# Interleaving two arrays in place: three large buffers, 32 KiB load rows and 64 KiB store rows

## The chip, the cores and the metric

One core of one Trainium2 chip runs the kernel; nothing else runs on the chip. The metric is the device time of an execution in microseconds (us). The profile's span is about 2 us shorter than that time (317.6 against 319.8 us for the kernel before). The experiments ran on several chips, each beside the kernel before, whose medians were 319.56 to 319.86 us. Its executions agree within 0.3%; those of some kernels below do not, which turns out to be part of the story.

## The reference

```python
batch, seq, dim = 32, 256, 1024          # x, y: fp32
result = np.zeros((batch, seq, dim * 2), dtype=np.float32)
result[..., 0::2] = x
result[..., 1::2] = y
```

As flat arrays, out[2i] = x[i] and out[2i+1] = y[i]. There are 67.11 MB to read and 67.11 MB to write, and no arithmetic.

## The kernel before

Loads of x and y go through one queue (issued by the engine SP), stores through another (issued by ACT). VectorE copies each input to every second element of a separate output tile. `P` is 128 partitions; each partition's part of a transfer is one contiguous row. The load rows hold 4096 elements (16 KiB), the store rows 2 x 2048 (16 KiB), and small tiles end the kernel.

```python
WL = 4096
WS = 2048
xpool = ctx.enter_context(tc.tile_pool(name="xp", bufs=3))
ypool = ctx.enter_context(tc.tile_pool(name="yp", bufs=3))
opool = ctx.enter_context(tc.tile_pool(name="op", bufs=6))
lwidths = [WL] * (total // P // WL - 1) + [2048, 1024, 512, 256, 256]
for lw in lwidths:
    ...                                   # tiles and access patterns
    nc.sync.dma_start(out=xtile, in_=xs)
    nc.sync.dma_start(out=ytile, in_=ys)
    soff = 0
    while soff < lw:
        ...
        nc.vector.tensor_copy(out=otile[:, 0::2], in_=xsub)
        nc.vector.tensor_copy(out=otile[:, 1::2], in_=ysub)
        nc.scalar.dma_start(out=os_, in_=otile)
        ...
```

Of the kernel before, what the change touches and what calls it, by code (L numbers as in the profile page):

```python
# [2 lines left out]

# [4 lines left out]


@with_exitstack
def kernel(
    ctx: ExitStack,
    tc: tile.TileContext,
    x: bass.AP,
    y: bass.AP,
    out: bass.AP,
):
    nc = tc.nc
    P = 128  # L20

    total = 1
    for s in x.shape:
        total *= s

    WL = 4096
    WS = 2048

    xf = x.rearrange("b s d -> (b s d)")
    yf = y.rearrange("b s d -> (b s d)")  # L30
    of = out.rearrange("b s d -> (b s d)")

    fp32 = mybir.dt.float32

    xpool = ctx.enter_context(tc.tile_pool(name="xp", bufs=3))
    ypool = ctx.enter_context(tc.tile_pool(name="yp", bufs=3))
    opool = ctx.enter_context(tc.tile_pool(name="op", bufs=6))

    lwidths = [WL] * (total // P // WL - 1) + [2048, 1024, 512, 256, 256]
    assert sum(lwidths) == total // P  # L40

    start = 0
    k = 0
    for lw in lwidths:
        xtile = xpool.tile([P, WL], fp32, name="xtile")[:, :lw]
        ytile = ypool.tile([P, WL], fp32, name="ytile")[:, :lw]

        xs = dataclasses.replace(xf, offset=start, ap=[[lw, P], [1, lw]])
        ys = dataclasses.replace(yf, offset=start, ap=[[lw, P], [1, lw]])
        nc.sync.dma_start(out=xtile, in_=xs)  # L50
        nc.sync.dma_start(out=ytile, in_=ys)  # L51

        soff = 0
        while soff < lw:
            width = min(WS, lw - soff)
            otile = opool.tile([P, 2 * WS], fp32, name="otile")[:, : 2 * width]
            os_ = dataclasses.replace(
                of,
                offset=2 * start + 2 * soff,
                ap=[[2 * lw, P], [1, 2 * width]],  # L60
            )
            xsub = xtile[:, soff : soff + width]
            ysub = ytile[:, soff : soff + width]
            if False:
                nc.gpsimd.tensor_copy(out=otile[:, 0::2], in_=xsub)
                nc.gpsimd.tensor_copy(out=otile[:, 1::2], in_=ysub)
            else:
                nc.vector.tensor_copy(out=otile[:, 0::2], in_=xsub)  # L68
                nc.vector.tensor_copy(out=otile[:, 1::2], in_=ysub)  # L69
            nc.scalar.dma_start(out=os_, in_=otile)  # L70
            k += 1
            soff += width

        start += P * lw
    assert start == total


# [1 line left out]
_INS = ['x', 'y']  # L79
_OUTS = [((32, 256, 2048), 'float32')]  # L80


# [23 lines left out]
```

## Time and profile before

| | before |
|---|---|
| time, median of runs | 319.79 us (319.71 to 320.22) |
| span of the profiled run | 317.6 us |
| rate over the span | 423 GB/s |
| VectorE busy | 76.8 us (24%) |
| DMA packets | 10,802 |

A page is read from the span down. "Busy" is an engine's own work. The line of digits for DMA is the mean busy share of sixteen DMA engines in 40 slices of the span, in tenths; the GB/s below counts bytes at the start of the packet that moves them, so with long packets single slices jump about (from 370 to 479 after the first and before the last slice of the changed kernel). The queue lines give packets, megabytes and the time of the packets as a share of sixteen engines' span; q1 carries the loads, q10 the stores. A packet here is one record of the trace: one row of a transfer, or a small one at its end (q1 of the kernel before has 5760, which is 40 loads of 128 rows and 16 small ones). The prediction shows these lines and reads them.

### The profile page before, as it was taken

How to read it: one execution, taken by the hardware profiler on the slowest of the kernel's cores; microseconds unless marked ns; L12 is line 12 of the kernel's file. 1: busy time of each engine (PE TensorE's matmuls, PEld its weight loads, DVE VectorE, ACT ScalarE, POOL GpSimd, SP SyncE). 2: the span in 40 equal slices, each digit the busy share in tenths (PEclk: the TensorE clock that was granted, in tenths of full speed). 3: DMA queues.
4: the chain of work that ended last, by engine and by line, in shares of the span. 5: the costliest groups of instructions: out<-in, count | busy, mean ns of one | idle time of the engine just before them, and what ended most of it. 6: DMA issues, size and time to landing. Idle time of an engine off the chain costs nothing.

```text
span 317.6 us, 285 instructions
## 1 busy us (share of the span) xinstructions
DVE 76.8 (24%) x70; POOL 0.2 (0%) x4
## 2 busy tenths in 40 slices
DVE  0522112222022221122220222202222202221130
POOL 0000000000000000000000000000000000000000
DMA  8999999999999999999999999999999999999997
GB/s 293 429 396 429 429 431 429 429 429 437 437 435 433 433 429 429 429 429 429 429 431 429 429 429 435 437 437 430 431 431 429 431 429 429 429 432 427 421 423 285
DMA packets 10802, 134.24 MB, mean 423 GB/s; under 512 B 1200, under 2 KB 1712, under 8 KB 2608
## 3 DMA queue, kind: packets, MB, share of 16 engines
q1 hardware_dynamic: 5760, 67.11, 50.0%
q10 hardware_dynamic: 5040, 67.11, 49.4%
q14 instruction: 2, 0.02, 0.0%
HBM read 67.11 MB, written 67.11 MB: 423 GB/s over the span
## 4 chain that ended last, share of the span: by engine, by line
DMA 94%; issue 3%; SPq 1%; DVE 1%
DMA xtile<-in_x_dram 82%; DMA ytile<-in_y_dram 12%; SPq L51 0%; DVE otile L69 0%; SPq L50 0%; DVE otile L68 0%
## 5 line engine op out<-in xcount | busy, mean ns | idle before, releaser
L68 DVE COPY otile<-xtile 128x2048 f32<-128x2048 f32 (+3 forms) x35 | 38.4, 1134 | 118.4 <-issue 94.4
L69 DVE COPY otile<-ytile 128x2048 f32<-128x2048 f32 (+3 forms) x35 | 38.4, 1134 | 117.9 <-DMA ytile<-in_y_dram 117.9
L90 POOL MEMSET const-bfloat16-1.0<- 128x1 bf16 x1 | 0.1, 102 | 0.0
L90 POOL MEMSET const-uint8-127<- 128x1 uint8 x1 | 0.1, 101 | 0.0
L90 POOL MEMSET const-float32-0.0<- 128x1 f32 x1 | 0.1, 99 | 0.2 <-issue 0.2
L90 POOL MEMSET const-float32-1.0<- 128x1 f32 x1 | 0.1, 98 | 0.0
## 6 DMA issues: line engine op xcount, KB each, us to landing
out_dram<-otile ACTq DMA_DIRECT2D x31, 2048.0 KB, 19.5
xtile<-in_x_dram SPq DMA_DIRECT2D x15, 2048.0 KB, 38.8
ytile<-in_y_dram SPq DMA_DIRECT2D x15, 2048.0 KB, 38.8
xtile<-in_x_dram SPq DMA_DIRECT2D x1, 1024.0 KB, 36.4
ytile<-in_y_dram SPq DMA_DIRECT2D x1, 1024.0 KB, 34.0
out_dram<-otile ACTq DMA_DIRECT2D x1, 1024.0 KB, 9.2
xtile<-in_x_dram SPq DMA_DIRECT2D x1, 512.0 KB, 29.0
ytile<-in_y_dram SPq DMA_DIRECT2D x1, 512.0 KB, 30.2
```

The source lines that it names most:

```text
L68: nc.vector.tensor_copy(out=otile[:, 0::2], in_=xsub)
L69: nc.vector.tensor_copy(out=otile[:, 1::2], in_=ysub)
L90: nc = _bacc.Bacc("TRN2", target_bir_lowering=False, num_devices=1)
```

## The change

The intent is fewer and longer transfers. A tile now has 8192 elements a partition, and one 64 KiB buffer holds x in its lower and y in its upper half, then the interleaved result. So that nothing is overwritten before it is read, half of x waits in PSUM and the rest is spread out in copies of halving length. Loads have rows of 32 KiB; a store has rows of 64 KiB, but for the last tile, which is stored in two halves.

```diff
-    WL = 4096
-    WS = 2048
+    W = 8192
+    H = W // 2
+    EDGE = 64
...
+    zpool = ctx.enter_context(tc.tile_pool(name="zp", bufs=3))
+    tpool = ctx.enter_context(tc.tile_pool(name="tp", bufs=1, space=bass.MemoryType.PSUM))
...
+        nc.sync.dma_start(out=z[:, :W], in_=xs)
+        nc.sync.dma_start(out=z[:, W:], in_=ys)
...
+        copy(out=keep, in_=z[:, H:W])                     # half of x to PSUM
+        hi = H
+        while hi > EDGE:
+            lo = hi // 2
+            copy(out=z[:, 2 * lo : 2 * hi : 2], in_=z[:, lo:hi])
+            hi = lo
...
+        copy(out=z[:, 1:W:2], in_=z[:, W : W + H])        # first half of y
...                                                        # second half of y, by halves
+        copy(out=z[:, W : 2 * W : 2], in_=keep)           # back from PSUM
...
+            os_ = dataclasses.replace(of, offset=2 * base, ap=[[2 * W, P], [1, 2 * W]])
+            nc.scalar.dma_start(out=os_, in_=z)           # 64 KiB rows
```

More of the change, by code (lines that the diff above doesn't have):

```diff
@@ L24 @@
         total *= s
-    WL = 4096
-    WS = 2048
+    n = total // (P * W)
+    assert n * P * W == total
     xf = x.rearrange("b s d -> (b s d)")
@@ L33 @@
     fp32 = mybir.dt.float32
-    xpool = ctx.enter_context(tc.tile_pool(name="xp", bufs=3))
-    ypool = ctx.enter_context(tc.tile_pool(name="yp", bufs=3))
-    opool = ctx.enter_context(tc.tile_pool(name="op", bufs=6))
-    lwidths = [WL] * (total // P // WL - 1) + [2048, 1024, 512, 256, 256]
-    assert sum(lwidths) == total // P
-    start = 0
-    k = 0
-    for lw in lwidths:
-        xtile = xpool.tile([P, WL], fp32, name="xtile")[:, :lw]
-        ytile = ypool.tile([P, WL], fp32, name="ytile")[:, :lw]
-        xs = dataclasses.replace(xf, offset=start, ap=[[lw, P], [1, lw]])
-        ys = dataclasses.replace(yf, offset=start, ap=[[lw, P], [1, lw]])
-        nc.sync.dma_start(out=xtile, in_=xs)
-        nc.sync.dma_start(out=ytile, in_=ys)
-        soff = 0
-        while soff < lw:
-            width = min(WS, lw - soff)
-            otile = opool.tile([P, 2 * WS], fp32, name="otile")[:, : 2 * width]
-            os_ = dataclasses.replace(
-                of,
-                offset=2 * start + 2 * soff,
-                ap=[[2 * lw, P], [1, 2 * width]],
-            )
-            xsub = xtile[:, soff : soff + width]
-            ysub = ytile[:, soff : soff + width]
-            if False:
-                nc.gpsimd.tensor_copy(out=otile[:, 0::2], in_=xsub)
-                nc.gpsimd.tensor_copy(out=otile[:, 1::2], in_=ysub)
-            else:
-                nc.vector.tensor_copy(out=otile[:, 0::2], in_=xsub)
-                nc.vector.tensor_copy(out=otile[:, 1::2], in_=ysub)
-            nc.scalar.dma_start(out=os_, in_=otile)
-            k += 1
-            soff += width
-        start += P * lw
@@ L75 @@
-    assert start == total
+    zpool = ctx.enter_context(tc.tile_pool(name="zp", bufs=3))
+    tpool = ctx.enter_context(tc.tile_pool(name="tp", bufs=1, space=bass.MemoryType.PSUM))
+    epool = ctx.enter_context(tc.tile_pool(name="ep", bufs=2))
+    copy = nc.vector.tensor_copy
+    for t in range(n):
+        z = zpool.tile([P, 2 * W], fp32, name="z")
+        base = t * P * W
+        xs = dataclasses.replace(xf, offset=base, ap=[[W, P], [1, W]])
+        ys = dataclasses.replace(yf, offset=base, ap=[[W, P], [1, W]])
+        nc.sync.dma_start(out=z[:, :W], in_=xs)
+        nc.sync.dma_start(out=z[:, W:], in_=ys)
+        keep = tpool.tile([P, H], fp32, name="keep")
+        edge = epool.tile([P, EDGE], fp32, name="edge")
+        copy(out=keep, in_=z[:, H:W])
[4 more added lines that the diff above has]
+            hi = lo
+        copy(out=edge[:, :hi], in_=z[:, :hi])
+        copy(out=z[:, 0 : 2 * hi : 2], in_=edge[:, :hi])
+        copy(out=z[:, 1:W:2], in_=z[:, W : W + H])
+        last = t == n - 1
+        if last:
+            os_ = dataclasses.replace(of, offset=2 * base, ap=[[2 * W, P], [1, W]])
+            nc.scalar.dma_start(out=os_, in_=z[:, :W])
+        k = 0
+        while H - k > EDGE:
+            k1 = k + (H - k) // 2
+            copy(
+                out=z[:, W + 2 * k + 1 : W + 2 * k1 : 2],
+                in_=z[:, W + H + k : W + H + k1],
+            )
+            k = k1
+        edge2 = epool.tile([P, EDGE], fp32, name="edge2")
+        copy(out=edge2[:, : H - k], in_=z[:, W + H + k : 2 * W])
+        copy(out=z[:, W + 2 * k + 1 : 2 * W : 2], in_=edge2[:, : H - k])
+        copy(out=z[:, W : 2 * W : 2], in_=keep)
+        if last:
+            os_ = dataclasses.replace(of, offset=2 * base + W, ap=[[2 * W, P], [1, W]])
+            nc.scalar.dma_start(out=os_, in_=z[:, W:])
+        else:
+            os_ = dataclasses.replace(of, offset=2 * base, ap=[[2 * W, P], [1, 2 * W]])
+            nc.scalar.dma_start(out=os_, in_=z)
```

## The prediction

> **What bounds the kernel now.** I read the page from the top. The span and the engine line come first, then the slices of DMA share and rate, then the queues, then the chain that ended last.
>
> ```profile
> span 317.6 us, 285 instructions
> DVE 76.8 (24%) x70; POOL 0.2 (0%) x4
> ...
> DMA  8999999999999999999999999999999999999997
> GB/s 293 429 396 429 429 431 429 429 429 437 437 435 433 433 429 429 429 429 429 429 431 429 429 429 435 437 437 430 431 431 429 431 429 429 429 432 427 421 423 285
> DMA packets 10802, 134.24 MB, mean 423 GB/s; under 512 B 1200, under 2 KB 1712, under 8 KB 2608
> ...
> q1 hardware_dynamic: 5760, 67.11, 50.0%
> q10 hardware_dynamic: 5040, 67.11, 49.4%
> ...
> DMA 94%; issue 3%; SPq 1%; DVE 1%
> ```
>
> The reader is to see three things. VectorE (DVE) works 24% of the time, so it is no bound. The DMA share is 9 in every slice but the first and last, and the two queues' packets fill 50.0% + 49.4% of sixteen engines: the engines never wait for work. And the rate is flat at 429 to 437 GB/s, so only the first and last slice, and the height of the plateau, can be improved. Bytes can't: 67.11 MB in and 67.11 MB out is what the task demands.
>
> How high is the plateau exactly? The chain in order of time repeats one wait:
>
> ```profile
> 38.31 38.84 DMA xtile<-in_x_dram
> ...
> 77.21 38.84 DMA xtile<-in_x_dram
> ```
>
> From 38.31 to 77.21 is 38.90 us, in which two x loads, two y loads and four stores of 2 MiB pass: 16.78 MB, so 431.3 GB/s.
>
> The packet records of the trace say where the rest goes. Their median durations by size are 46 ns (1 KiB), 84 (2 KiB), 159 (4 KiB), 309 (8 KiB), 611 (16 KiB), the same for both queues. That is a straight line: (611 - 46) / 15,360 bytes gives 27.2 GB/s for each engine, plus about 9 ns for each packet. The 4-byte records (1200 of them, "under 512 B" above, 16 for each of the 75 transfers) take 9 ns each. So one row of a tile is one packet, and a transfer also has one small completion packet per engine. Successive packets overlap a little: in the 38.90 us each engine moves 1.0486 MB, 38.55 us at 27.2 GB/s, with 64 row packets and 8 completions; the left-over 0.35 us over 72 packets is 4.9 ns each. I use 4.9.
>
> The budget of the span, then: 134.22 MB at 16 x 27.2 = 435.2 GB/s is 308.4 us. Packets: 10,800 / 16 = 675 an engine x 4.9 ns = 3.3 us. Together 311.7. The other 5.9 us are the ends. The stretches 0 to 2 and 2 to 38.3 us show 115 and 412 GB/s, 15.2 MB, worth 35.2 us at 431.3: the head costs 3.1 us (first bytes at 1.73 us, then a slow start). The tail has 2.8: the last y load lands at 312.7, one small copy follows, the bulk of the bytes is out by 315.2, and the completion and the end follow.
>
> [...] In the kernel before, both queues' packets are 16 KiB and each queue has half of the time (50.0% and 49.4%)[...]
>
> **The change part by part.**
>
> 1. *Larger rows.* Loads go from 16 to 32 KiB rows and stores from 16 to 64. Loads: 16 transfers of 128 rows. Stores: 7 of 128 rows of 64 KiB and 2 of 128 rows of 32 KiB. That is 2048 + 1152 row packets and 25 x 16 completions, 3600 packets instead of 10,800, or 225 an engine: 1.1 us instead of 3.3. This gains **2.2 us**, all on the bounding resource. That is all the larger rows can give, as the bytes already move at the ceiling.
>
> 2. *VectorE.* The copies by form of the kernel before:
>
> ```profile
> L69 DVE COPY otile<-ytile 128x2048 f32<-128x2048 f32 x31 | 36.7, 1225 | 110.6 <-DMA ytile<-in_y_dram 110.6
> L69 DVE COPY otile<-ytile 128x1024 f32<-128x1024 f32 x1 | 0.7, 697 | 0.9 <-DMA ytile<-in_y_dram 0.9
> L69 DVE COPY otile<-ytile 128x512 f32<-128x512 f32 x1 | 0.4, 429 | 0.2 <-DMA ytile<-in_y_dram 0.2
> ```
>
> They give 0.16 us + n/1920 us for n elements. Now per tile of 8192: 4096 into PSUM[...] 4.43; x halves of 2048 down to 64 and two edge copies 1.23 + 0.69 + 0.43 + 0.29 + 0.23 + 0.19 + 0.39 = 3.45; y's first half 2.29; y's second half 3.45 again; from PSUM 4.43. Sum 18.05 us a tile, 144 us in all, about twice before but under half the span. It stays hidden as a sum. As a latency it counts: after the y load has landed, 2.29 + 3.45 + 4.43 = 10.2 us, with some 0.5 us (a guess) for instructions that wait for one another 10.7. With [...]issue to first byte (1.0: 0.73 to 1.73 in the trace) a store starts 13.2 us after the last byte of its loads.
>
> 3. *Buffers.* Three of 64 KiB are both input and output. A load of tile t+3 waits for the store of tile t. Does the DMA run dry? I walk it at 433.7 GB/s (134.22 MB in 308.4 + 1.1 us), where a tile alone loads in 19.3 us. If a store packet of 64 KiB alternates with a load packet of 32, a store gets two thirds: 29.0 us, while loads advance half a tile. Store 0 starts at 3.1 + 19.3 + 13.2 = 35.6, with 14.1 MB of loads done; it ends at 64.6. Store 1 starts at 67.3, then 113, 145, 190, 222, 268. Loads meanwhile are at 18.3 MB at 64.6, 23.7 at 96, 35.1 at 142, 40.4 at 174, 51.9 at 219, 57.2 at 251, and tiles freed by the stores allow 25.2, 33.6, 41.9, 50.3, 58.7 and 67.1 at the same ends, so loads always have some left when a store ends. Where stores pause (2.6 or 17 us in turn) loads run alone at the full rate, as x and y of the first tiles did before (landings at 8.48 and 13.35: 2.1 MB in 4.87 us, 431 GB/s). **No idle time in the middle.** An equal split of bytes gives the same.
>
> 4. *The end.* The taper of small tiles is gone. By the walk loads end at 286, when store 6 still has 7 us to go (to 293.2). The last y lands at 287.6; its first half may be stored from 287.6 + 2.3 + 1.0 = 290.9, before store 6 has ended, and takes 9.7 us to 302.9; the second is ready at about 299. So the DMA stays full to the last byte, with margins of 2.3 and 3.6 us, and the end is the last byte plus about 2.4 us (before: 315.2 to 317.6). The tail gains **0.4 us**.
>
> Sum: 3.1 + 308.4 + 1.1 + 2.4 = 315.0 us of span. The measured time before is 2.2 above the span (319.8 against 317.6): 317.2.
>
> **The rivals.** (a) *The end runs dry.* If the chain of dependent copies takes longer, or store 6 is out sooner, the DMA idles between the last load and the last tile's stores; 10.7 us is the whole of it, and 2 to 6 us the likely loss: 319 to 323. For it: no copy before reads or overwrites what another copy made, so the cost of dependence is not seen. Against: two margins and the split last store. (b) *Waits on whole buffers.* If x and y, now halves of one buffer, are told apart no more, the y load waits for the x load and the last half store holds up the copies behind it: 325 to 330. The split of the last store would then make no sense, so I doubt it. (c) *VectorE becomes the bound*: it would need over 38.9 us a tile against 18; no. (d) *Larger rows raise the ceiling itself*: the straight line of the packets speaks against it; with no packet cost at all the floor is bytes and ends alone, 3.1 + 308.4 + 2.4 + 2.2 = 316.1. (e) *Large packets do worse*, by uneven progress of the engines or stores alone being slower than loads, as the last 26 us have stores only, never seen before: 1 to 3 us.
>
> **Range and chances.** The sum says 317.2. Downwards there is at most about 1 us to the floor and some in the head and tail; upwards (a) and (e) give a few us. So 315.3 to 321.0. Faster by over 2% means under 313.4, below the floor of the bytes: 0.03. Slower by over 2% means over 326.2, rival (b) or (a) at its worst: 0.06. Within 2%: 0.91.
>
> **What would show it.** Right: about 3600 packets; packets of 32 KiB at 1214 ns and of 64 KiB at 2418; plateau near 434 GB/s; DMA share 9 from the second slice to the last but one; PSUM copies near 4.4 us; first store near 35 us; VectorE near 144 us. Wrong: slices with DMA under 9 near 290 us (a); y loads issued only after x landed (b); a plateau under 431 (e).

## The result, and the profile after

The changed kernel took 329.27 us (median of four, 326.71 to 332.65), against 319.75 for the kernel before: 2.7% slower, the ratio being 1.027 (95% interval 1.022 to 1.033). A ratio here is the mean time of one kernel's fast runs over that of the other's in the same rounds, so it is not quite the ratio of the medians. The fourth run, 332.65, counts as slow and is left out of the ratio; on one core that mark only means more than 1.5% above the fastest run (its granted clock is 1.0 as in the others), and the scatter itself, 1.8% where the kernel before has 0.2%, is a finding.

The page of the changed kernel:

```profile
span 325.9 us, 249 instructions
DVE 141.3 (43%) x152; POOL 0.2 (0%) x4
...
DMA  8999999999989999999999999999999899998994
...
DMA packets 3601, 134.23 MB, mean 412 GB/s; under 512 B 400, under 2 KB 400, under 8 KB 400
...
q1 hardware_dynamic: 2304, 67.11, 49.5%
q10 hardware_dynamic: 1296, 67.11, 48.6%
```

Two thirds of the packets are gone, as intended, and the DMA engines are still nearly always busy: 49.5% + 48.6% = 98.1% of 325.9 us is 319.7 us of packets an engine, where the kernel before had 99.4% of 317.6, or 315.7. At the prediction's 4.9 ns a packet, fewer packets for the same bytes should have taken less time; they took 4.0 us an engine more. The engines are busy but slower. The windows of the stretch in which loads and stores run beside each other say the same (columns: from and to in us, length, VectorE busy and its instructions, GpSimd busy and its, granted clock of TensorE, mean DMA share, GB/s):

```profile
34.00:277.00 243.00, 105.69 (x115) 0.00 (x0) 1.00 1.00 420
```

The DMA share is 1.00 and the rate 420 GB/s, where the kernel before has 431 over its plateau.

The records of single packets name it. I call a packet slow when it takes over 5% more than the median of its size, and add up what all packets take beyond that median, divided by sixteen engines:

```
packets            number  median ns  mean ns   slow   beyond the median, us an engine
32 KiB loads         2048       1213     1260    201   5.97
64 KiB stores         896       2418     2478    130   3.38
32 KiB stores         256       1213     1216      0   0.06
sum                                                    9.4    (kernel before: 1.8)
```

At their medians the packets would take (2304 x 1213 + 896 x 2418 + 400 x 9) ns / 16 = 310.3 us; the slow ones add 9.4, and the other 6.2 us of the span an engine has no packet. Where one queue was alone there are next to none: of the loads, 16 in the first 34 us (as the very first packets) and one from 100.0 to 114.5, 185 to 196 and 266 to 277 us together; of the stores, none from 299 us on. **The slow packets come where both queues run.** The 25 slow loads from 34 to 38 us come while the first store, issued at 32.87, is being taken up; the clean kernels have such a burst too (e2 below: 34 slow loads from 26 to 32 us).

The second loss is at the end. The timeline of the changed kernel, with the start, the length, the engine, what it did, and in brackets how long the engine had been idle and for what. The first line merges the seven 64 KiB-row store issues:

```profile
32.87 243.60 ACTq L87 DMA_DIRECT2D out_dram<-z  x7
...
298.53 2.29 DVE L63 COPY z<-z 128x4096 f32<-128x4096 f32 x1 [14.47 <-DMA z<-in_y_dram]
...
300.86 0.34 ACTq L67 DMA_DIRECT2D out_dram<-z  x1
...
308.70 0.34 ACTq L84 DMA_DIRECT2D out_dram<-z  x1
```

The last y load has landed at 298.5 us, 11 us after the predicted 287.6. The trace has sixteen landings for each transfer, one for each engine's part, and the copy that needs this load starts with the last of them. They run from 279.7 to 298.5 us: the first engine was done 19 us before the last. I call this the spread of a landing; in the kernel before, the widest in any transfer is 1.7 us. Near the end, DMA shares fell:

```profile
290.00:300.00 10.00, 1.47 (x1) 0.00 (x0) 1.00 0.95 413
300.00:310.00 10.00, 8.46 (x10) 0.00 (x0) 1.00 0.88 380
310.00:322.00 12.00, 0.00 (x0) 0.00 (x0) 1.00 0.93 401
```

VectorE is innocent. Its copies took what had been predicted, those with PSUM among them (4.43 and 4.42 us), and its chain after a landing was 22.70 to 32.87 us in the first tile, 10.2 us:

```profile
L52 DVE COPY keep<-z 128x4096 f32<-128x4096 f32 x8 | 35.4, 4428 | 64.6 <-DMA z<-in_x_dram 64.4
L63 DVE COPY z<-z 128x4096 f32<-128x4096 f32 x8 | 18.4, 2296 | 99.5 <-DMA z<-in_y_dram 99.5
L81 DVE COPY z<-keep 128x4096 f32<-128x4096 f32 x8 | 35.3, 4418 | 0.0
```

### The profile page after: what moved, and what is told of

It is laid out like the page before. It is cut to its first block, busy times and chain, and to the rows that moved or that the text cites. A ratio compares the mean times of both kernels' runs of the same rounds, so it can differ in the third digit from the quotient of the medians.

```text
span 325.9 us, 249 instructions
## 1 busy us (share of the span) xinstructions
DVE 141.3 (43%) x152; POOL 0.2 (0%) x4
## 2 busy tenths in 40 slices
DMA packets 3601, 134.23 MB, mean 412 GB/s; under 512 B 400, under 2 KB 400, under 8 KB 400
## 3 DMA queue, kind: packets, MB, share of 16 engines
q1 hardware_dynamic: 2304, 67.11, 49.5%
q10 hardware_dynamic: 1296, 67.11, 48.6%
## 4 chain that ended last, share of the span: by engine, by line
another core or an unknown queue 46%; DVE 33%; issue 7%; DMA 7%; DVEq 1%; SPq 0%
DVE z L81 9%; DVE z L72 8%; DVE z L58 7%; DMA z<-in_y_dram 7%; DVE z L63 6%; DVE keep L52 3%; DVEq L113 1%; DVE z L79 0%; DVE z L61 0%; DVE edge L60 0%; DVE edge L78 0%; SPq L46 0%; DVEq L52 0%
## 5 line engine op out<-in xcount | busy, mean ns | idle before, releaser
L52 DVE COPY keep<-z 128x4096 f32<-128x4096 f32 x8 | 35.4, 4428 | 64.6 <-DMA z<-in_x_dram 64.4
L63 DVE COPY z<-z 128x4096 f32<-128x4096 f32 x8 | 18.4, 2296 | 99.5 <-DMA z<-in_y_dram 99.5
L81 DVE COPY z<-keep 128x4096 f32<-128x4096 f32 x8 | 35.3, 4418 | 0.0
L72 DVE COPY z<-z 128x2048 f32<-128x2048 f32 (+5 forms) x48 | 24.6, 512 | 1.4
L58 DVE COPY z<-z 128x2048 f32<-128x2048 f32 (+5 forms) x48 | 24.6, 512 | 1.4
L79 DVE COPY z<-edge 128x64 f32<-128x64 f32 x8 | 1.6, 197 | 0.3
L61 DVE COPY z<-edge 128x64 f32<-128x64 f32 x8 | 1.6, 197 | 0.3
L78 DVE COPY edge<-z 128x64 f32<-128x64 f32 x8 | 1.5, 188 | 0.0
L60 DVE COPY edge<-z 128x64 f32<-128x64 f32 x8 | 1.5, 184 | 0.0
```

The costliest lines, as they stand in the source:

```text
L52: copy(out=keep, in_=z[:, H:W])
L58: copy(out=z[:, 2 * lo : 2 * hi : 2], in_=z[:, lo:hi])
L60: copy(out=edge[:, :hi], in_=z[:, :hi])
L61: copy(out=z[:, 0 : 2 * hi : 2], in_=edge[:, :hi])
L63: copy(out=z[:, 1:W:2], in_=z[:, W : W + H])
L72: copy(out=z[:, W + 2 * k + 1 : W + 2 * k1 : 2], in_=z[:, W + H + k : W + H + k1],)
```

## The experiments

The question is why packets turn slow and the engines drift apart. The theories:

- **A**: rows at power-of-two distances in memory make the engines collide.
- **B**: the packets of the two queues are unlike, so loads crawl at one third beside stores, the stores run out, start again, and the engines drift.
- **C**: long packets do it by themselves.
- **D**: few, coarse transfers do it, with loads and stores starting and stopping.

### First four: one property each

**e1: tiles of 7296 (and one of 7168) elements, nothing else.**

```diff
-    W = 8192
+    WIDTHS = [7296] * 8 + [7168]
```

> The changed kernel with tiles of 7296 elements (8 of them, and one of 7168) in place of 8192: load rows of 28.5 KiB, store rows of 57 KiB, so that rows of one transfer no longer lie a power of two apart in memory; all else stays, the 2:1 of the row sizes too. Theory A (rows at power-of-two distances make the DMA engines collide in memory): the slow packets, 331 of 3200 in the changed kernel and worth 9.4 us an engine, nearly vanish (under 2 us), and the time falls to 316 to 320. Theories B (unlike packet sizes of loads and stores), C (long packets) and D (few, coarse transfers with changing regimes): slow packets stay at 6 us an engine or more, time 325 to 333.

It took 336.83 us (336.3 to 338.7), the ratio 1.053, with 12.3 us of slow packets an engine and landing spreads of up to 28.7 us. Theory A is refuted: other row distances made it worse.

**e2: each store as two transfers of 32 KiB rows.**

```diff
-            os_ = dataclasses.replace(of, offset=2 * base, ap=[[2 * W, P], [1, 2 * W]])
-            nc.scalar.dma_start(out=os_, in_=z)
+            SP = 2 * W // 2
+            for j in range(2):
+                os_ = dataclasses.replace(of, offset=2 * base + j * SP, ap=[[2 * W, P], [1, SP]])
+                nc.scalar.dma_start(out=os_, in_=z[:, j * SP : (j + 1) * SP])
```

> The changed kernel with every 8 MiB store cut into two transfers of 32 KiB rows, issued together: load and store packets are then equal. Theory B (unlike packet sizes make loads crawl at one third and the engines drift apart): the spread of a load's landings over the engines, up to 19 us in the changed kernel, falls under 5 us, slow packets under 3 us an engine, time 317 to 321. Theories A, C and D: little change, 324 to 333.

It took 317.25 us (317.01 to 317.61), the ratio to the kernel before 0.9925 (0.991 to 0.994). This one edit takes away the whole loss and beats both kernels, the one before by 0.75%. Its page, and its window of the stretch with both queues:

```profile
span 315.2 us, 267 instructions
...
DMA  8999999999999999999999999999999999999996
...
q1 hardware_dynamic: 2304, 67.11, 49.8%
q10 hardware_dynamic: 2304, 67.11, 49.3%
```

```profile
36.00:285.00 249.00, 113.68 (x123) 0.00 (x0) 1.00 1.00 434
```

Not one of its 2048 store packets is slow, slow loads cost 1.6 us an engine, 50 of the 54 at the start and where stores first join (before 36 us), the widest landing spread is 2.1 us, and the plateau is 434 GB/s. The last y load landed at 289.1. Against the changed kernel (span 325.9) the span is 10.7 us shorter: 9.4 - 1.6 = 7.8 fewer of slow packets, 6.2 - 2.8 = 3.4 fewer without a packet, and 0.5 more for the extra packets at their medians.

**e3: all transfers in 16 KiB rows**, as columns of the same tiles (x, y, and the result each cut along the row, two transfers a load and four a store).

> The changed kernel with all transfers cut to rows of 16 KiB (columns of the same tiles), so the packets are those of the kernel before while tiles, buffers, copies and row distances stay. Theory C (long packets) and B: slow packets vanish, and the time is 317 to 320 (packet cost back, 2 us). Theory A (row distance): slow packets stay, 324 to 333. Theory D (coarse transfers, changing regimes): slow packets stay in part where loads and stores start again, and the end is late: 321 to 328.

319.07 us (318.98 to 319.16): slow packets 1.9 us, widest spread 1.7 us. In place, through PSUM and with three large buffers the traffic is as steady as before, so these are not the cause. It is 1.8 us behind e2, with 288 more packets an engine: by that an estimate of 6.3 ns a packet, near the 4.9 of the prediction.

**e4: tiles of 4096 in six buffers**, rows of 16 KiB beside 32.

```diff
-    W = 8192
+    W = 4096
...
-    zpool = ctx.enter_context(tc.tile_pool(name="zp", bufs=3))
-    tpool = ctx.enter_context(tc.tile_pool(name="tp", bufs=1, space=bass.MemoryType.PSUM))
+    zpool = ctx.enter_context(tc.tile_pool(name="zp", bufs=6))
+    tpool = ctx.enter_context(tc.tile_pool(name="tp", bufs=2, space=bass.MemoryType.PSUM))
```

> The changed kernel with tiles of 4096 in six buffers of 32 KiB: load rows of 16 and store rows of 32 KiB, still 2:1, in place and through PSUM as before. Theory D (few, coarse transfers): loads and stores run more evenly, the last tile's latency halves, time 316 to 320. Theory B (2:1): slow packets and drift stay, 322 to 330.

325.22 us (323.82 to 325.61), slow packets 6.2 us, spreads up to 16.8 us. Tiles of half the size took off 4 of the 12 us that e2 took off, so D alone is refuted; with no packet over 32 KiB most of the loss is still there.

### The kernel before with unlike rows, and the other way round

**e5: the kernel before with one size changed.**

```diff
-    WS = 2048
+    WS = 4096
...
-    opool = ctx.enter_context(tc.tile_pool(name="op", bufs=6))
+    opool = ctx.enter_context(tc.tile_pool(name="op", bufs=3))
```

> The kernel BEFORE with one size changed: its output tiles hold 4096 elements of x and y in place of 2048 (three of 32 KiB in place of six of 16 KiB, the same memory), so its stores have rows of 32 KiB while its loads keep 16. No in-place work, no PSUM, separate buffers. Theory B (unlike packet sizes of the two queues are enough): slow packets of 3 us an engine or more, landing spreads over 5 us, and a time of 322 to 330, against 319.6. Rival D' (unlike sizes hurt only with the in-place buffers and their few transfers): packets stay at 611 and 1213 ns, time 317 to 321.

324.60 us (323.91 to 325.60), the ratio 1.0155: 5.6 us of slow packets, spreads up to 18.8 us. Its queues have 5760 and 2880 packets for the same bytes. The loss has been given to the kernel before by its store rows. Against that kernel e4, e5 and e7 stay within 2% (ratios 1.011 to 1.017), but their 95% intervals are clear of 1.

**e6: e1 with each store cut in two**, so rows of 28.5 KiB on both sides (the edit of e2 on top of e1).

> The 7296-element tiles of e1 (336.8 us, with 12.3 us of slow packets an engine) with each store cut in two, so loads and stores both have rows of 28.5 KiB. Theory B: slow packets fall under 2.5 us an engine and the time to 316.5 to 319. If the odd row length itself were to blame for e1, it stays above 325.

317.62 us (317.53 to 318.79), slow packets 1.7 us, widest spread 2.2 us. The worst of all rows, at 336.8, becomes nearly as good as e2.

**e7: each store as four transfers of 16 KiB rows**, loads at 32 KiB (the edit of e2 with 4 for 2).

> The changed kernel with each store cut in four transfers of 16 KiB rows (the last tile stays as it is), loads at 32 KiB: now the loads' packets are twice the stores'. Theory B in its general form (any unlike sizes): slow packets and spreads as in the changed kernel, 321 to 333 us. Narrow form B2 (only stores that outrun the loads do harm, as loads then crawl and stores run out): no drift, 317 to 321.

323.26 us (322.77 to 323.59), slow packets 3.5 us, spreads up to 11.0 us. Unlike sizes hurt this way round too, if less.

The traces of the kernels so far show one more difference. In each one with the loss, one queue runs dry, with no packet on any engine, again and again in the middle: the stores' queue in the changed kernel (three times for 14.5 to 19.1 us), in e1 (three times for 13.7 to 18.5 us), in e4 (seven times for 7.2 to 9.8 us) and in e5 (seven times for 6.9 to 7.9 us), and the loads' queue in e7 (five times for 7.9 to 11.0 us). In e2, e3 and e6 neither queue has such a gap of 2 us, and in the kernel before only the small tiles at the end have one, of 2.7 us. So a stop and restart of a queue is a rival that these seven experiments cannot part from unlike rows. It cannot be all of it: in e1 19 packets were slow from 55 to 86 us, before the first dry spell.

### A rig of bare transfers: sizes and restarts apart

The next kernels give a wrong result on purpose. They load x and y into buffers that nobody reads and store from one buffer of constants, so that nothing but the transfers is left. "Steady": the buffer is filled once, and both queues were meant to be busy from 20 us on until one ends; in e8 and e9 this held only up to 166 us, as is seen below. "Restarts": VectorE fills the buffer anew before each 8 MiB store, so the store queue has no packet for 18 to 24 us and starts again, seven times.

```python
for t in range(n):
    ...                                          # access patterns os_ and s_
    z = spool.tile([P, 2 * W], fp32, name="z")   # restarts: one buffer, filled for each store
    nc.vector.memset(z, float(t))                # steady: once, before the loop
    nc.scalar.dma_start(out=os_, in_=z)          # or cut into 2 or 4 column pieces
    for src in (xf, yf):
        ld = lpool.tile([P, W], fp32, name="ld") # 4 buffers (e13, e16: 2 of 64 KiB)
        nc.sync.dma_start(out=ld, in_=s_)        # or cut into 2
```

**e8 and e9: steady, 32 beside 64 KiB** (the same kernel twice).

> Wrong result on purpose: the same loads of 32 KiB rows into four buffers that nobody reads, and the same stores of 64 KiB rows from one constant buffer, with no wait between the two queues, so both run side by side from 20 us until the stores end near 235 us, then loads alone. If alternating packets of 32 and 64 KiB are harmful as such: slow packets all along, more than 5 us an engine, load landings spreading over 5 us. If only the stops and restarts of a queue do the harm: all packets at 1213 and 2418 ns after the start, spreads under 4 us, span near 314 us.

> Wrong result on purpose: the same kernel as e8, which showed no slow packets beyond the start in its profile (span 314.8) but 322.9 us in one of its two timings. If undisturbed 2:1 traffic is harmless, most runs lie at 316 to 318 and the profile again has under 2 us of slow packets an engine. If 322 to 323 comes up in a third of the runs or more, unlike sizes do harm without any restart of a queue, only not always.

e8's profile shows perfect traffic: span 314.8, slow packets 1.7 us, no spread over 0.6. Its load issues, each released by the landing of an earlier load, show how the queues share:

```profile
55.17 0.33 SPq L46 DMA_DIRECT2D ld<-in_x_dram  x1
...
84.23 0.33 SPq L46 DMA_DIRECT2D ld<-in_y_dram  x1
113.17 0.33 SPq L46 DMA_DIRECT2D ld<-in_x_dram  x1
```

A 4 MiB load takes 29.0 us here, which is one third of 434 GB/s: a turn was one row, as the records from 60 to 63 us show sixteen load rows, then sixteen store rows, and the 32 KiB rows got one third beside the 64 KiB rows (35.9% of the engines' time from 60 to 75 us, the stores 64.5%), as the prediction had it. But e8's second timing was 322.9, and e9 ran 20 times: 316.4 to 330.2 us, and once 357.4. Twelve of the twenty are over 322 and count as slow; of the eight fast ones four lie at 320.2 to 320.4, where e10 below stays under 317.1.

e9's own profile (a span of 322.1 us, counted slow) begins like e8's, with spreads of at most 0.7 us for what landed up to 139 us and 1.0 up to 169. Then they grow, to 3.8 us in the transfer that landed at 191, 8.2 at 232 and 15.9 at 274. Of the 72 slow packets after 36 us all but one come from 178 us on. By then the traffic was no longer steady, in either run: from the sixth on, each store came too late, issued only with the landing of an earlier load (169.25, 209.56 and 250.75 us in e9; what it waited for is not on record), and the store queue had no packet from 166.4 to 172.7, 202.2 to 213.6 and 243.3 to 255.0 us. So these two runs do not show that unlike sizes do harm without a restart. While both queues were fed, up to 166 us, both profiles are clean. After the restarts one execution drifts, and the other, with restarts of the same kind, has not one slow packet after 36 us.

**e10: steady, 32 beside 32.**

> Wrong result on purpose: as e9 with each store cut in two transfers of 32 KiB rows: equal packets, both queues always busy until one ends. All theories: under 2 us of slow packets, 316 to 318 us, in every run within 1 us.

Four runs of 316.62 to 317.08 us, spreads of 0.5 us at most. Its store queue never runs dry for over 2.0 us. This bare transfer is also a measure for e2: at 317.25 the interleaving costs it half a microsecond.

**e11 to e15 and e17: restarts.**

> Wrong result on purpose: as e9 (loads of 32 KiB rows that nobody gates, stores of 64 KiB rows), but before each 8 MiB store VectorE fills the one store buffer anew, which it may only do when the last store has landed: the store queue runs dry for some 16 us and starts again, seven times. If restarts do the harm, alone or with unlike sizes: 4 us or more of slow packets an engine, landing spreads over 3 us. If restarts are harmless: under 2.5 us, spreads under 2 us. The time itself says nothing, as the stores now wait.

> Wrong result on purpose: e11 with each store cut in two transfers of 32 KiB rows. Restarts alone do the harm: slow packets as in e11, 4 us or more an engine. Only the two together do: under 2.5 us an engine and spreads under 2 us here, while e11 has more.

> Wrong result on purpose: e11 (stores of 64 KiB rows, the store queue running dry before each store) with the loads also in rows of 64 KiB (8 MiB each, two buffers). If unlike sizes are the cause: like e12, under 3.5 us of slow packets an engine and landing spreads under 5 us (one packet is 2.4 us). If long packets do the harm by themselves: 6 us or more and spreads over 7 us, as in e11 (12.1 us, spreads up to 34 us). The time itself says nothing.

> Wrong result on purpose: the rig of e11 and e12 (store queue runs dry before each 8 MiB store) with loads in rows of 16 and stores in rows of 32 KiB. Theory B (unlike sizes do harm by themselves): over 4 us of slow packets an engine and spreads over 4 us. Theory C' (only packets of 64 KiB do): under 3 us, as in e12 (2.5).

> Wrong result on purpose: the same rig with loads in rows of 32 and stores in rows of 16 KiB. Theory B: over 4 us of slow packets an engine. Theory C': under 3 us. Narrow form B2 (only stores longer than loads do harm): under 3 us here, over 4 in e14.

> Wrong result on purpose: the rig of e12 with rows of 16 KiB on both sides, the sizes of the kernel before. All theories: under 2.5 us of slow packets an engine, spreads under 2.5 us.

**e16: steady, 64 beside 64.**

> Wrong result on purpose: e13 without its restarts: loads and stores in rows of 64 KiB, both queues always busy, equal shares. If the harm of 64 KiB packets needs a restart: 316 to 318 us in every run, under 3 us of slow packets an engine. If long packets do harm in steady traffic too: times scattered over several us as in e9 (316.4 to 330), slow packets over 4 us.

```
rows, load/store   restarts: slow us an engine, widest spread     steady (e9: to 166 us): times
16 / 16   (e17)     2.5     1.5 us
32 / 32   (e12)     2.5     2.4 us                                 e10: 316.6 to 317.1 (4 runs)
16 / 32   (e14)     3.5     9.7 us
32 / 16   (e15)     4.6     2.6 us
32 / 64   (e11)    12.1    34.1 us                                 e9:  316.4 to 330.2, one 357.4 (20 runs)
64 / 64   (e13)    11.3    39.0 us                                 e16: 318.0 to 322.6 (12 runs)
```

The times of the runs with restarts (373 to 419 us) mean nothing, as their stores wait. The pair e11 and e12 differs by the store rows (and so the size of a store) alone, and both first stores begin at the same moment, when the buffer is filled: 12.1 us against 2.5. e13 was a miss: like sizes of 64 KiB should have been clean under B and are as bad as 32 beside 64. So theory C holds too, for 64 KiB. e14 lies under the 4 us that B wanted, with a spread well over it; e15 lies over it with hardly any spread. In this rig unlike rows of at most 32 KiB do a little harm; in the real kernels e4, e5 and e7 they do more, 3.5 to 6.2 us. e16 shows that 64 KiB rows on both sides scatter the times even in steady traffic, though its one profile had only 2.5 us of slow packets; its spreads grew to 6.4. Here the store queue never ran dry for over 4.4 us. The mean over sixteen engines hides what happened: in the last transfer fourteen parts landed from 313.0 to 313.5 us, one at 316.5 and one at 319.3. Two engines had fallen behind, and the last one set the time.

**e18: e2 with the halves of each store issued in the other order.** e2's trace had shown its first store issue at 25.0 us, where the changed kernel's was at 32.9: a first half need not wait for the copies into the second. This run was to hold it back.

```diff
-            for j in range(2):
+            for j in (1, 0):
```

> As e2, but the store of the second half is issued first and that of the first half behind it on the same queue, so no store of a tile (but the last) starts before the tile's last copy, as in the changed kernel: the first store issue is near 32.9 us. If the row size is what matters: 316.5 to 319 us, under 3 us of slow packets an engine. If the earlier start of the stores was: 322 to 333 us.

317.23 us (316.93 to 317.92), but the first store was again issued at 24.95 us: this was evidently the first half's store, as in e2, since the copies into the second half run until 32.8 us. So the run tells nothing of the earlier start. Two others do: e7's first store also went out at 25.1 us and a loss was there, so an early start is not enough; and e11 against e12 shows the effect of the row size with no difference in the first start. That the early start has no share at all in e2's gain is not shown.

## Why the prediction was wrong, point by point

- **Larger rows gain 2.2 us: the count and the medians right, the cost wrong.** There are 3601 packets, their medians are 1213 and 2418 ns (1214 and 2418 predicted), and in e2 the sum comes out: 315.0 and 0.3 for its 63 more packets an engine, against a span of 315.2 us. But "1.1 us instead of 3.3" takes every packet at its nominal time. The 32 KiB loads and 64 KiB stores took 1260 and 2478 ns in the mean, and all packets together 9.4 us an engine beyond their medians, 7.8 more than in e2. The terms 308.4 + 1.1 = 309.5 us of packets an engine measured 319.7.
- **VectorE: right.** 141.3 us in all (144 predicted), 4.43 and 4.42 us for a copy of 4096 into PSUM and out of it (4.43 predicted, which no trace of the kernel before showed; within SBUF the same size took 2.30, so PSUM copies ran at about half the rate), 10.2 us from landing to store (10.7). The half microsecond guessed for dependence was not needed. The walk's 13.2 us from the last byte to a store also hold an estimate for the landing that the author took from no trace; in the trace of the kernel before, a landing comes 0.35 us (median) after the small packet at the end of its part.
- **"No idle time in the middle": the step that failed.** The DMA share did stay near 1.00 in the middle, so idle time is not what went wrong. The walk moved all engines as one fluid at 433.7 GB/s, which is the same assumption as the nominal packet above. Measured with both queues in play were 420 GB/s, and loads that landed over up to 19 us: the engines did not stay together. Other parts of the walk came true: the two-to-one share is what e8 shows up to 142 us, and the pauses of the stores, 2.6 or 17 us in turn, measured 2.3 to 3.4 and 14.5 to 19.1. It gave them no cost.
- **The end: wrong for the same reason.** The last y load landed at 298.5, not 287.6, since this landing waited for the slowest engine (its parts landed from 279.7 to 298.5 us). The margins of 2.3 and 3.6 us were worked out for engines in step. The time without a packet grew by 3.4 us against e2, where that load landed at 289.1.
- **The rivals.** (b) and (c) did not occur: all first six loads were issued within 3.7 us, and VectorE was busy for 43%. (a) occurred, as a consequence. (e), "large packets do worse, by uneven progress of the engines", names what happened, and its sign, a plateau under 431, came true; but it was given 1 to 3 us and cost about 11. Its other half, that stores alone are slow, is wrong: from 299 us on no packet was. The prediction gave slower by over 2% a chance of 0.06, by way of (b) or (a) and not (e).
- **The sentence "An equal split of bytes gives the same"** misled too. The walk gives the same result for both; measured are 315.2 us of span with equal rows (e2) and 325.9 with 64 beside 32.
- **A reading of the page was too smooth.** "Flat at 429 to 437 GB/s" leaves out the third slice (396) and three of the last (421 to 427). Nothing in the sum rests on it.

What is shown: cutting the store rows to the load rows' 32 KiB removes the loss (e2: 317.25 us against 329.27), equal rows do so for other tiles (e6: 317.62 against 336.83), and unlike rows bring it into the kernel before (e5: 324.60 against 319.81). Rows of 64 KiB did harm even where both sides had them (e13: 11.3 us of slow packets an engine; e16, with both queues fed: times of 318.0 to 322.6). A restart of the store queue alone, with rows of 16 or 32 KiB on both sides, did little (2.5 us of slow packets in e12 and e17, 1.8 in e10).

What stays open: how much of the changed kernel's loss belongs to the length and how much to the unlikeness, as its stores are both; how far unlike rows need a queue that runs dry and restarts, as in the losing kernels the two came together; whether it is the rows or the whole transfers, since every transfer has 128 rows and the two sizes changed together in each run; and what holds a single packet up when the engines are out of step, which no record here shows.

## What to carry to other kernels

When two DMA queues run side by side at the rate of this case (434 GB/s over 249 us in e2), try rows of one size, and of 16 or 32 KiB rather than 64. Here 8 MiB stores in 64 KiB rows gave 326.7 to 332.7 us, and the same bytes in 4 MiB stores of 32 KiB rows 317.0 to 317.6 (e2); the length of a row changed with the size of the transfer. The longer rows saved some nanoseconds a packet (6.3 by the estimate from e3 and e2) and cost over ten microseconds (a span of 325.9 against 315.2 us). Look beyond the median packet and the busy share: compare the mean with the median (1260 and 1213 ns for the loads here), and the first engine's landing with the last's (19 us apart). A scatter of 1 or 2% between runs (1.8% in the changed kernel), where the kernel before agreed within 0.3%, was a sign of it here.
